# Where attention's last transposes go in PSUM, and behind which copies a gate_up weight's high part is cut, in a hybrid attention block on one core

## The chip, the cores and the metric

The kernel runs on one core of a Trainium2 chip. A core has a matrix engine (PE, whose weight loads are listed apart as PEld), a vector engine (DVE), a scalar engine (ACT), a general engine (POOL), a sync engine that issues DMAs (SP), and 16 DMA engines. PE writes only to PSUM, which has eight banks of 128 partitions by 512 f32; DVE and ACT read it back. Each engine runs its own list of instructions in order and waits for the others by semaphores.

The metric is the device time of one execution in microseconds (us). A number of executions is timed and their median taken; one more execution is recorded by the hardware profiler, and all the rows below come from it.

## What is computed

One layer on x of 1024 rows by 1024 columns, in f32. What matters here is:

```python
q, k, v, f_logit, g_b, g_c, hc, gate_conv, gate_attn = jnp.split(h @ w_in, _SPLITS, axis=-1)
ya = g_b * causal_depthwise_conv(g_c * hc, conv_w)
yb = forgetting_attention(q, k, v, log_sigmoid(f_logit + b_f))   # 8 heads of 64, causal softmax with a bias
merged = sigmoid(gate_conv) * (ya @ w_branch[0]) + sigmoid(gate_attn) * (yb @ w_branch[1])
x = x + rmsnorm(merged @ w_out, norm_mix_post)
h = rmsnorm(x, norm_ffn_pre)
g, u = jnp.split(h @ w_gate_up, 2, axis=-1)
x = x + rmsnorm((silu(g) * u) @ w_down, norm_ffn_post)
```

## The kernel before, in words

**Products.** PE multiplies f32 as three products of split operands: `split(hi, lo, src)` has ACT copy `src` to a rounded high part `hi` and DVE subtract it from `src` to give `lo`; `mm3` then issues high by high, high by low and low by high. The large products (w_in, w_out, gate_up, w_down) are Strassen-Winograd products of seven half-size ones; `prod` is one of them, 12 matmuls of 128x512 for 128 columns of a weight.

**Order.** Up to line 1385 (`strict[0] = ()`) attention runs in the order in which it is written, on all engines: `InOrder` keeps each instruction behind the one written before it on its engine. After that line a planner orders each engine's instructions, by its own times and by priorities. There, `pinned(call, names...)` (line 118) has the instructions that `call` issues on the named engines kept behind whatever was written last before them on the same engine; nothing else is held by it, and instructions written later may still be planned ahead. `ahead(call)` (line 124) raises a priority. All operations pass through one helper, so every row names line 76 and rows are told apart by their tiles.

**Attention.** `steps` (line 898) are 24 steps, each a pair of heads and one or two blocks of 128 query rows; `NU` is 24. Step t multiplies queries and keys into PSUM tiles `sp` (pool `pss`, tag "S", two buffers of two banks, `qk`), DVE adds the bias and takes the row's extreme (`row_max`), and ACT takes the exponential (`expo`, tile `pt`). One step later `turn_bank(back, e, half, engine)` (line 871) transposes the blocks of head e on PE, up to four into one bank of `tps` (tag "T", two buffers of one bank), and returns a `drain`, the copy of that bank to `ptT` by ACT or DVE. After another step or more `pv_pair` multiplies `ptT` with the values into `po`. The remaining two banks are `ma` (holds `po`) and `mb`. Between these, `fill` gives PE matmuls of the other branch (`pba`, `branch_a`): 12 matmuls per tile, all into the one bank `mb`, which DVE empties by a multiplication into `um`. `units` says how many quarters of such a tile each step takes; step 24 takes a whole one. In the loop at line 1278, step 24 has no queries left: it issues `fills()` (12 matmuls, and ACT's high part of a w_branch weight), then the transposes of step 23 (query block 4, five key blocks for each of two heads), and step 25 multiplies steps 22 and 23 with the values.

**w_out's product and the start of gate_up.** From line 1618 the four row pairs i = 0 to 3 of w_out are multiplied (`first`, `second`, `p_s2`, `p_s1`, `p_s3`, `p_s4`, `p_a22`), normalised (`e_norm(i)`, DVE and ACT, which writes `tt` and the tile of `keeps[i]`, named `raw` for i < 3) and transposed (`e_turn(i)`, line 1595: 16 transposes on PE in four banks `tp`, kept in their place behind the PE instruction written before them, and four ACT copies `um<-tp`). `psm` has four banks at this stage, shared by `tp`, `q` and `b3`. `p_s3(i)` ends in an ACT copy `c<-p`, a DVE addition to `c` and an ACT square of it (`junk<-c`). In the last turn of the loop, i = 3, `e_turn(1)` is written right behind `p_s3(3)`.

The first gate_up products are begun in the same stage: `f_begin(n, ...)` (line 1629) loads weight n (`raw`, three buffers, SP's DMA queue), splits it (`prep_first`, line 565) and multiplies it with the first quarter of the turned rows; `f_end(n)` does the second quarter. They are written as begin 0, `e_turn(2)`, begin 1, end 0, begin 2, end 1, begin 3, `e_turn(3)`, end 2, end 3 (lines 1702 to 1711).

Of the kernel before, what the change touches and what calls it, by code (L numbers as in the profile page):

```python
# [10 lines left out]
F32 = mybir.dt.float32  # L11
# [6 lines left out]
P = 128  # L18
S = 1024
# [3 lines left out]
NC = 512  # L23
# [23 lines left out]
def block_kernel(  # L47
# [17 lines left out]
    engines = ("tensor", "vector", "scalar", "gpsimd", "sync")  # L65
# [28 lines left out]
    def pool(name, bufs=1, side="left", space=None):  # L94
        kw = dict(name=name, bufs=bufs)
        if space is not DRAM:
            kw["reuse_waits"] = "tile"
        if space is not None:
            kw["space"] = space
        else:  # L100
            kw["side"] = side
        stack = ExitStack()
        ctx.callback(stack.close)
        return stack.enter_context(tc.tile_pool(**kw)), stack.close

    def f32(ap):
        return ap.bitcast(F32)
# [4 lines left out]
    def sub(o, a, b):  # L112
        nc.vector.tensor_tensor(o, a, b, op=ALU.subtract)
# [4 lines left out]
    def pinned(call, *names):  # L118

        was, strict[0] = strict[0], names  # L120
        call()
        strict[0] = was

    def ahead(call, by=80):
        with tc.high_priority(offset=by):
            call()

    def copy(o, a):
        nc.scalar.activation(o, a, AF.Copy)

    def split(hi, lo, src):

        copy(hi, src)
        sub(lo, src, f32(hi))
# [9 lines left out]
    cpool, _ = pool("const")  # L144
    stat, _ = pool("stat", 4, side="right")
    stat.tile([P, 56], F32, name="pad", bufs=1)
    dpool, _ = pool("dram", space=DRAM)
# [383 lines left out]
    wpool, _ = pool("w")  # L531
# [4 lines left out]
    def kblk(t):  # L536
        return t.rearrange("p (a b) -> p a b", b=P)
# [4 lines left out]
    def raw_t():  # L542
        return wtile("raw", 3)

    def hi_t():
        return wtile("hi", 4, F32R)

    def lo_t():
        return wtile("lo", 3, F32R)
# [10 lines left out]
    def kmaj(src):  # L560
        return src.rearrange("(k p) m -> p k m", p=P)

    LO, UP = slice(0, 4), slice(4, 8)

    def prep_first(src1, there=None):

        if there is None:
            r1 = raw_t()
            nc.sync.dma_start(r1, kmaj(src1))
            h1, l1 = hi_t(), lo_t()  # L570
            split(h1, l1, r1)
        else:
            r1, h1, l1 = there
        return dict(A11=(h1[:, LO], l1[:, LO]), A12=(h1[:, UP], l1[:, UP])), r1
# [113 lines left out]
    def wcols(c0):  # L688
        return win[:, c0 : c0 + P]
# [178 lines left out]
            accum_out=rsums[steps[t][0]][:, c : c + 1],  # L868
        )

    def turn_bank(t, e, half, engine):

        n = sum(i + 1 for i in steps[t][1])
        ks = range(4 * half, min(4 * half + 4, n))
        if not ks:
            return
        if (t, e) not in ptTs:
            ptTs[t, e] = (
                t1.tile([P, ST, P], F32, tag="pT", name="ptT", bufs=6)
                if t  # L880
                else raw_t()
            )
        tps = pss.tile([P, 4, P], F32, tag="T", name="tps", bufs=2)
        for k in ks:
            nc.tensor.transpose(
                tps[:, k - ks[0], :], ps_[t, e][:, k * P : (k + 1) * P], ident
            )
        o, a = ptTs[t, e][:, ks[0] : ks[-1] + 1, :], tps[:, : len(ks), :]

        def drain():  # L890
            if engine == "ACT":
                copy(o, a)
            else:
                nc.vector.tensor_copy(o, a)

        return drain
# [3 lines left out]
    NU = len(steps)  # L900
# [95 lines left out]
    for ij, (kind, j, _, _) in enumerate(jobs):  # L996
        mid = None
        if ij in side:
            cut, store = side.pop(ij)
# [7 lines left out]
        if ij < 2:  # L1007
            if ij == 0:
                r1 = raw_t()
                nc.sync.dma_start(r1, kmaj(wcols(jobs[1][2])))  # L1010
                t0_.tile([P, S], F32, tag="p", name="room", bufs=2)
                h1, l1 = (
                    kblk(t0_.tile([P, S], F32R, tag="cb", name=n, bufs=2)) for n in ("h1", "l1")
                )
# [8 lines left out]
            w = {**w, **prep_rest(wcols(jobs[ij][3]), r1)}  # L1023
            if ij == 1:
                pairs.q.append(pairs.prep(*pairs.srcs.popleft()))
            _, c12, c21, c22 = strassen(w, h1b, psm, pp, p1, mid)
# [7 lines left out]
        else:  # L1034
            w = pairs.get()
            psm_close()
            strict[0] = engines
            pss, pss_close = pool("pss", space=PSUM)
# [11 lines left out]
        elif kind == "gb":  # L1050
            for m, parts in ((j, (c11, c12)), (j + 1, (c21, c22))):
                zt = zts.pop(m)
                for n in range(2):
# [5 lines left out]
                    for t in (1, 0):  # L1059
                        back = 2 - t  # L1060
# [29 lines left out]
    um = um_pool.tile([P, KT, S], F32, name="um")  # L1090
# [78 lines left out]
    def inverse(j):  # L1169

        invs[j] = st_tile("ri", 2 * ST)
        nc.vector.reciprocal(invs[j], rsums[j])
# [78 lines left out]
    cuts, at = defaultdict(list), defaultdict(list)  # L1251
# [32 lines left out]
    for t in range(2, NU + 2):  # L1284
        turned = None
        now = groups(t) if t < NU else ([], [])
        back = t - 1 if t <= NU else None
        wide = back and sum(i + 1 for i in steps[back][1]) > 6
        if t < NU:
            step_qk(t)  # L1290
        if t > 6:
            for u in due(t):
                pv_pair(u)
        if t in rows:
            turned = inverse_rows(rows[t], pst, "mb")
        if t == NU + 1:
            turned = inverse_rows(3, pss, "T", 2)
        lows, muls = [], []

        def fills():  # L1300
            lows.extend(f for f in (g() for g in cuts.pop(t, ())) if f)
            muls.extend(m for m in (next(fill, None) for _ in range(units.get(t, 0))) if m)

        if t == NU:
            fills()
        if back:
            da = turn_bank(back, 0, 0, "ACT")
            db = turn_bank(back, 0, 1, "DVE")
            da()
        if t <= 6:  # L1310
            for u in due(t):
                pv_pair(u)
        for i, e in now[0]:
            row_max(t, i, e)
        if t < NU and len(steps[t][1]) > 1:
            mask_of(t, steps[t][1][1])
        if turned:
            turned()
        if t == NU:
            for f in lows + muls:  # L1320
                f()
            lows, muls = [], []
        if back and db:
            db()
        for i, e in now[0]:
            expo(t, i, e)
        if t == NU:
            inverse(3)
        else:
            fills()  # L1330
        if back:
            dc = turn_bank(back, 1, 0, "ACT" if wide else "DVE")
            dd = turn_bank(back, 1, 1, "DVE" if wide else "ACT")
        for i, e in now[1]:
            row_max(t, i, e)
        if 7 < t < NU:
            for m in muls:
                m()
            muls.clear()
        if t == NU - 1:  # L1340
            for i, e in now[1]:
                expo(t, i, e)
        if back:
            dc()
            if dd:
                dd()
        if t < NU - 1:
            for i, e in now[1]:
                expo(t, i, e)
        if t + 1 < NU:  # L1350
            mask_of(t + 1, steps[t + 1][1][0])
        for f in lows + muls + at.pop(t, []):
            f()
# [241 lines left out]
    def e_turn(i):  # L1595
        for e in range(2):
            st = 2 * i + e
            ss = slice(st * P, (st + 1) * P)
            for q in range(2):
                tp = psm.tile([P, 4, P], F32, tag="mm", name="tp")  # L1600

                def turns():
                    for k in range(4):
                        kt = 4 * q + k
                        nc.tensor.transpose(
                            tp[:, k, :], turned[i][e][:, kt * P : (kt + 1) * P], ident
                        )

                pinned(turns, "tensor")
                ahead(lambda: copy(um[:, 4 * q : 4 * q + 4, ss], tp))  # L1610

    for step in (0, 1, 2, 3):
        first(step)
# [5 lines left out]
    for k in (0, 2):  # L1619
        w = ep.tile([P, D], F32, tag="t", name="wr", bufs=1)  # L1620
        cut_wo(w, ((B22, 4 + k, n2), (B22, 5 + k, n2)))

    def f_src(f):
        return wgu[:, f * P : (f + 1) * P], wgu[:, FH + f * P : FH + (f + 1) * P]

    FIRSTS = [*range(2, NPRE), 0, 1]
    begun, kept = {}, {}

    def f_begin(n, b1, p1):
        f = FIRSTS[n]  # L1630
        w, _ = prep_first(f_src(f)[0])
        prod(b1, w["A11"], hb[B11], True)
        pinned(lambda: copy(p1, b1), *(("scalar",) if n >= 8 else ()))
        if f > 1:
            nc.gpsimd.dma_start(pre_dram[f][0], p1)
        begun[n] = w, b1, p1

    def f_end(n, c11):
        f = FIRSTS[n]
        w, b1, p1 = begun.pop(n)  # L1640
# [82 lines left out]
    def first_tile(n, name, slot):  # L1723
        f = FIRSTS[n]
        return um[:, slot, (n1, n2)[f]] if f < 2 else t_(fp, name)

    for n in range(4, NPRE + 1):
# [6 lines left out]
        if n == 8:  # L1734
            for sl in range(4):
                a = slice(sl * P, (sl + 1) * P)
                b = slice(NC + sl * P, NC + (sl + 1) * P)
# [28 lines left out]
    for f in range(NF):  # L1766
        if f < NPRE:
# [7 lines left out]
            _, g2, u1_, u2 = strassen(rest.get(False), hb, psm, fp, p1, rest.more)  # L1775
# [35 lines left out]
    def cut(t, g):  # L1811

        return t[:, : min(2, NK - 2 * g)]
# [237 lines left out]
```

## Time and profile before

| | us |
|---|---|
| median of 3 executions | 1319.41 |
| lowest and highest of them | 1319.0, 1319.99 |
| the profiled execution | 1319.29 |
| its span, first to last instruction | 1317.2 |

The page of the profile gives the busy time of each engine over the span, and other views of the same recording give single instructions in order of time, the total of waits by engine, and the busy time by stretches of the span. A row of the timeline has the start in us, the length in us, the engine, the operation, the tile written and the tiles read (`out<-in`), the shape, the number of instructions merged in the row, and in brackets the idle time of the engine before it and what ended that. Matmuls are pipelined, so their rows overlap: the time that a matmul costs is the distance to the next start, not its length.

### The profile page before, as it was taken

Reading aid. Unit: us, or ns where it says so; the run is one execution under the profiler, and the core shown is the slowest. Engines: PE = TensorE matmul, PEld = TensorE weight load, DVE = VectorE, ACT = ScalarE, POOL = GpSimd, SP = SyncE. Lnnn points to the kernel's source line nnn. Section 1 sums busy time; section 2 is a strip of 40 time slices with the busy share of each in tenths; the row PEclk is TensorE's granted clock in tenths of the full one; section 3 lists DMA queues with packets and bytes.
Section 4 is the critical chain, followed back from the end, with each engine's and each line's share of the span. In section 5 each row is a group of like instructions: output and inputs, shape, how many; then the busy total and the mean of one; then the engine's idle time right before and its main releaser. Section 6 shows DMA issues by size and latency. Waiting matters only on the chain.

```text
span 1317.2 us, 17978 instructions
## 1 busy us (share of the span) xinstructions
PE 1306.7 (99%) x6710; PEld 1089.5 (83%) x6710; DVE 964.9 (73%) x1514; ACT 556.8 (42%) x895; POOL 142.4 (11%) x271
## 2 busy tenths in 40 slices
PE   9999999999999999999999999999999999999998
PEld 8988888888888888888888888888888888888886
DVE  6974878765656876686798788987766776676685
ACT  6642322243355866514577522322322234444452
POOL 0001000011012212020011021221001110000000
PEclk9999999999999999999999999999999999999999
DMA  6344544555536545465266455553223338866441
GB/s 217 113 120 136 150 123 121 153 164 146 152 120 200 161 144 171 152 232 208 76 228 207 153 168 177 176 184 104 97 88 118 106 111 282 317 249 193 158 168 64
DMA packets 189351, 211.00 MB, mean 160 GB/s; under 512 B 11584, under 2 KB 137600, under 8 KB 189264
## 3 DMA queue, kind: packets, MB, share of 16 engines
q1 hardware_dynamic: 155872, 146.64, 35.6%
q0 software_dynamic: 16496, 54.83, 11.2%
q10 hardware_dynamic: 16896, 8.39, 2.1%
q8 instruction: 52, 0.85, 0.3%
q14 instruction: 35, 0.29, 0.1%
HBM read 151.30 MB, written 58.52 MB: 159 GB/s over the span
## 4 chain that ended last, share of the span: by engine, by line
PE 96%; DVE 2%; ACT 1%; DMA 1%; issue 0%; SPq 0%; DVEq 0%; ACTq 0%
PE b L76 57%; PE pd L76 16%; PE pba L76 3%; PE pbb L76 3%; PE pv L76 3%; PE po L76 3%; PE tps L76 3%; PE p L76 2%; PE sp L76 2%; PE ma L76 1%; PE q L76 1%; PE tp L76 1%; PE mb L76 1%; DMA xt<-in_x_dram 1%; DVE t L76 0%
## 5 line engine op out<-in xcount | busy, mean ns | idle before, releaser
L76 PE MATMUL b<-x,hi 128*128 128x512 f32 x1088 | 335.3, 389 | 0.0
L76 PEld LDWEIGHTS b<-x,hi 128*128 128x128 f32 x1088 | 204.2, 188 | 42.1
L76 PE MATMUL b<-x,lo 128*128 128x512 f32 x544 | 211.7, 389 | 0.0
L76 DVE TENSOR_TENSOR c<-c,b 128x512 f32<-128x512 f32 x193 | 131.5, 681 | 62.2 <-PE b L76 54.7
L76 DVE TENSOR_TENSOR lo<-raw,hi 128x1024 fp32r<-128x1024 f32 x92 | 110.7, 1204 | 76.6 <-PE b L76 66.8
L76 ACT ACTIVATE hi<-raw 128x1024 fp32r<-128x1024 f32 (+1 forms) x99 | 100.6, 1018 | 97.3 <-PE b L76 49.8
L76 PEld LDWEIGHTS b<-x,lo 128*128 128x128 f32 x544 | 102.1, 188 | 21.2
L76 ACT ACTIVATE hi<-sx 128x1024 fp32r<-128x1024 f32 (+1 forms) x43 | 44.8, 1043 | 152.5 <-PE b L76 144.8
L76 ACT ACTIVATE sgf<-c 128x512 f32<-128x512 f32 x31 | 19.6, 633 | 131.9 <-DVE c L76 112.8
L76 DVE TENSOR_TENSOR lo<-sx,hi 128x1024 fp32r<-128x1024 f32 (+1 forms) x43 | 51.5, 1198 | 30.6 <-PE b L76 27.3
L76 DVE TENSOR_TENSOR sx<-raw 128x512 f32<-128x512 f32 x78 | 53.5, 687 | 14.4 <-DMA raw<-in_w_gate_up_dram 7.1
L76 PE MATMUL pd<-hi,lo 128*128 128x512 f32 x160 | 62.3, 389 | 0.0
L76 PE MATMUL pd<-hi 128*128 128x512 f32 x160 | 61.9, 390 | 0.0
L76 PE MATMUL pd<-ghi 128*128 128x512 f32 x148 | 57.6, 390 | 0.0
L76 PE MATMUL pd<-glo,ghi 128*128 128x512 f32 x148 | 57.6, 389 | 0.0
L76 PE MATMUL pd<-ghi,glo 128*128 128x512 f32 x148 | 57.6, 389 | 0.0
L76 PE MATMUL b<-hT34h,lo 128*128 128x512 f32 x136 | 52.9, 389 | 0.0
L76 PE MATMUL b<-hT34h,hi 128*128 128x512 f32 x136 | 52.9, 389 | 0.0
L76 PE MATMUL b<-hT34l,hi 128*128 128x512 f32 x136 | 52.9, 389 | 0.0
L76 PE MATMUL b<-hT12h,hi 128*128 128x512 f32 x136 | 52.9, 389 | 0.0
L76 PE MATMUL b<-hT12l,hi 128*128 128x512 f32 x136 | 52.9, 389 | 0.0
L76 PE MATMUL b<-hT12h,lo 128*128 128x512 f32 x136 | 52.9, 389 | 0.0
(425 smaller groups left out, 3015.4 us busy)
## 6 DMA issues: line engine op xcount, KB each, us to landing
raw<-in_w_gate_up_dram SPq DMA_DIRECT2D x55, 512.0 KB, 3.9
raw<-in_w_in_dram SPq DMA_DIRECT2D x35, 512.0 KB, 4.3
a_dramS<-um POOLq DMA_DIRECT2D x44, 256.0 KB, 3.0
a_dramA<-um POOLq DMA_DIRECT2D x33, 256.0 KB, 2.7
sg<-sg_dram SPq DMA_DIRECT2D x32, 256.0 KB, 3.9
x<-wo_dram SPq DMA_DIRECT2D x16, 512.0 KB, 5.8
graw<-a_dramS SPq DMA_DIRECT2D x14, 512.0 KB, 4.4
sg_dram<-c POOLq DMA_DIRECT2D x24, 256.0 KB, 3.4
```

Source lines behind the costliest of these rows:

```text
L76: ins = getattr(self.engine, name)(*args, **kw)
```

## The change

Two things are changed. In step 24 of attention the transposes of step 23 are written ahead of the 12 matmuls of `fills()`; for each head their two banks are the two halves of a tile of the tag "S" and no longer two tiles of the tag "T"; all four copies are written behind `fills()`; DVE's reciprocal (`inverse(3)`) is written behind them, and the multiplication that empties `mb` and the low part of the w_branch weight behind that. In w_out's stage, the four copies of `e_turn(1)` are pinned on ACT, and so is the split of gate_up's weight n = 1 (its high part alone is on ACT).

```diff
-    def prep_first(src1, there=None):
+    def prep_first(src1, there=None, cut=split):
...
-            split(h1, l1, r1)
+            cut(h1, l1, r1)
...
-    def turn_bank(t, e, half, engine):
+    def turn_bank(t, e, half, engine, at_=None):
...
-        tps = pss.tile([P, 4, P], F32, tag="T", name="tps", bufs=2)
+        if at_ is None:
+            tps = pss.tile([P, 4, P], F32, tag="T", name="tps", bufs=2)
+        else:
+            tps = at_[:, half].rearrange("p (a b) -> p a b", a=4)
...
         if t == NU:
+            lasts = []
+            for e, engines in enumerate((("ACT", "DVE"), ("DVE", "ACT"))):
+                two = pss.tile([P, 2, NC], F32, tag="S", name="tps2", bufs=2)
+                lasts += [turn_bank(back, e, half, eng, two) for half, eng in enumerate(engines)]
             fills()
+            for f in lasts:
+                f()
+            inverse(3)
+            for f in muls + lows + at.pop(t, []):
+                f()
+            continue
...
-        if t == NU:
-            for f in lows + muls:
-                f()
-            lows, muls = [], []
...
-        if t == NU:
-            inverse(3)
-        else:
-            fills()
+        fills()
...
-                ahead(lambda: copy(um[:, 4 * q : 4 * q + 4, ss], tp))
+                pinned(
+                    lambda: ahead(lambda: copy(um[:, 4 * q : 4 * q + 4, ss], tp)),
+                    *(("scalar",) if i == 1 else ()),
+                )
...
+    cuts_ = {1: lambda *a: pinned(lambda: split(*a), "scalar")}
...
-        w, _ = prep_first(f_src(f)[0])
+        w, _ = prep_first(f_src(f)[0], cut=cuts_.get(n, split))
```

## The prediction

> **What bounds the kernel now.** I read the page first, then busy time by stretches, then PE's waits, then the timeline of each engine around the two places that the diff touches.
>
> ```profile
> span 1317.2 us, 17978 instructions
> ...
> PE 1306.7 (99%) x6710; PEld 1089.5 (83%) x6710; DVE 964.9 (73%) x1514; ACT 556.8 (42%) x895; POOL 142.4 (11%) x271
> ```
>
> ```profile
> 646.00:700.00 54.00, 53.47 (x267) 44.20 (x266) 49.82 (x86) 38.72 (x76) 9.70 (x18) 1.00 0.66 223
> 700.00:1101.00 401.00, 401.00 (x1771) 332.12 (x1770) 310.18 (x441) 129.46 (x177) 55.19 (x102) 1.00 0.43 139
> ```
>
> ```profile
> PE tps L76 <- ACT ptT L76: 0.6, 1, 0.6
> PE tp L76 <- ACT um L76: 0.5, 1, 0.5
> ```
>
> PE is busy for 1306.7 of 1317.2 us. The columns of a stretch are its length, then busy time of PE, PEld, DVE, ACT, POOL, and the granted clock, which is 1.00. From 700 to 1101 us PE never stands. So the end is PE's list of matmuls plus the few places where it stands, and whatever is saved or lost ahead of 700 us arrives at the end undiminished. The two waits sit exactly where the diff is: transposes of attention that wait for a drain by ACT, and turned rows that wait for ACT's copy. The whole of it is one or two us, so this is an account of tenths.
>
> **Part 1: the last transposes.** PE, in order of time:
>
> ```profile
> 530.83 0.88 PE L76 MATMUL tps<-ident,pt 128*128 128x128 f32 x6
> 531.46 0.48 PE L76 MATMUL pba<-yh,s4h 128*128 128x512 f32 x1
> ...
> 534.32 0.82 PE L76 MATMUL tps<-ident,pt 128*128 128x128 f32 x6
> 535.26 0.50 PE L76 MATMUL pba<-yh,s4h 128*128 128x512 f32 x1
> ...
> 538.12 0.71 PE L76 MATMUL tps<-ident,pt 128*128 128x128 f32 x5
> 539.40 0.77 PE L76 MATMUL tps<-ident,pt 128*128 128x128 f32 x5 [0.58 <-ACT ptT L76]
> 540.10 2.62 PE L76 MATMUL po<-ptT,v 128*64 128x128 f32 x44
> ...
> 542.68 0.47 PE L76 MATMUL pba<-yh,s4h 128*128 128x512 f32 x1
> ```
>
> From the last transposes of step 22 (534.32) to the matmuls of step 25 (542.68) PE takes 8.36 us. Two stands lie in it. The 12 `pba` matmuls could not begin until DVE had emptied the single bank `mb` (six transposes elsewhere take 0.63 us to the next matmul, 530.83 to 531.46; here it is 0.94). And the five transposes of the second head waited for the drains of the first, since the tag "T" has two banks: 1.28 us from 538.12 to 539.40 for five transposes.
>
> After the change the list is: 6 transposes, 10 transposes, 12 `pba`, 44 `po`. By starts: 0.63 for the six; ten at 0.63/6 = 0.105 each, 1.05; the twelve 2.86 (535.26 to 538.12); the forty-four 2.58 (540.10 to 542.68). Sum 7.12, gain 1.24. With the slowest pace for transposes in these rows, 0.70 for five (539.40 to 540.10), ten cost 1.40 and the gain is 0.89. If only the idle time that the rows name goes, it is 0.58 and the 0.12 between the end of the transposes (534.32 + 0.82) and 535.26, 0.70 in all. I take 1.0, between the two paces, and keep 0.7 to 1.24.
>
> The Trainium skill, page Perfetto Trace Analysis, section on the Tensor Engine instruction, says that a matmul's end is estimated by the profiler and only its start observed; by that the idle column is a lower bound and the sum by starts the right one. By the idle column the first part would give 0.7, by starts 0.9 to 1.24; no row here decides between them.
>
> What could take the place of these stands? DVE and ACT at that time:
>
> ```profile
> 534.07 0.19 ACT L76 ACTIVATION_READ_ACCUMULATOR pt<-pt,nm 128x1 f32 x1
> ...
> 535.45 1.05 ACT L76 ACTIVATE hi<-raw 128x1024 fp32r<-128x1024 f32 x1
> ```
>
> ```profile
> 534.51 0.69 DVE L76 TENSOR_TENSOR um<-sg,pba 128x512 f32<-128x512 f32 x1 [1.61 <-PE pba L76]
> ...
> 536.32 0.68 DVE L76 TENSOR_TENSOR yb<-yb,rb 128x512 f32<-128x512 f32 x1
> ```
>
> The new transposes need step 23's exponentials. The last ends at 534.26; PE gets there at 534.32 + 0.63 = 534.95, so the cover of the 12 matmuls isn't needed. The two "S" tiles were freed by DVE even earlier, ahead of those exponentials. `mb` is empty at 535.20, the `pba` matmuls now start near 536.0: that stand goes. The drains are written behind the high part of the w_branch weight: ACT ends it at 536.50 and copies two banks by 537.4; DVE ends its division at 537.0 and copies its two by 537.9, then the reciprocal. `po` needs them at 538.9 or later: a cover of one us; without it each tenth would be PE's. What is late next is DVE's multiplication out of `mb`, which now waits for the `pba` matmuls behind the reciprocal, at 539.1 to 539.8; `mb` is wanted again at 541.7, and behind it on DVE stand one low part (1.2 us) and a division (0.7), done by 541.7, when the turned reciprocals arrive. One DMA is issued about a us later, the gate's second half, which takes the buffer that this multiplication frees; its first reader is a sigmoid behind step 25. Everything behind moves forward with PE.
>
> **Part 2: the weight's high part.** PE, then ACT, then DVE:
>
> ```profile
> 654.31 1.03 PE L76 MATMUL tp<-ident,raw 128*128 128x128 f32 x8
> ...
> 656.06 0.70 PE L76 MATMUL p<-x,hi 128*128 128x512 f32 x2
> ...
> 669.80 1.03 PE L76 MATMUL tp<-ident,raw 128*128 128x128 f32 x8
> ...
> 671.79 0.66 PE L76 MATMUL tp<-ident,tt 128*128 128x128 f32 x4 [0.53 <-ACT um L76]
> 672.21 0.71 PE L76 MATMUL p<-x,hi 128*128 128x512 f32 x2
> ...
> 683.82 1.06 PE L76 MATMUL tp<-ident,tt 128*128 128x128 f32 x8
> ```
>
> ```profile
> 669.71 1.07 ACT L76 ACTIVATE hi<-raw 128x1024 fp32r<-128x1024 f32 x1 [3.11 <-DMA raw<-in_w_gate_up_dram]
> 670.68 0.57 ACT L76 ACTIVATE c<-p 128x512 f32<-128x512 f32 x1
> 671.15 2.05 ACT L76 ACTIVATE um<-tp 128x512 f32<-128x512 f32 x4
> 673.06 0.66 ACT L76 ACTIVATE junk<-c 128x512 f32<-128x512 f32 x1
> ...
> 684.49 1.09 ACT L76 ACTIVATE um<-tp 128x512 f32<-128x512 f32 x2
> ```
>
> ```profile
> 670.81 1.23 DVE L76 TENSOR_TENSOR lo<-raw,hi 128x1024 fp32r<-128x1024 f32 x1
> 671.95 0.68 DVE L76 TENSOR_TENSOR c<-c,b 128x512 f32<-128x512 f32 x1
> ...
> 679.08 1.22 DVE L76 TENSOR_TENSOR lo<-raw,hi 128x1024 fp32r<-128x1024 f32 x1
> ...
> 685.28 1.28 DVE L76 SCALAR_TENSOR_TENSOR keep<-keep,r,gpo 128x1024 f32<-128x1024 f32 x1
> ...
> 688.28 0.74 DVE L76 SCALAR_TENSOR_TENSOR tt<-c,r,gpo 128x512 f32<-128x512 f32 x1
> ```
>
> ACT's list had the high part of weight 1 ahead of `c<-p` and the copies of `e_turn(1)`. Its DMA landed at 669.7, so the copies were late; with `b3` in one of the four banks, the fourth group of transposes had to wait for the first copy. The same 16 transposes took 1.75 us for pair 0 (654.31 to 656.06) and 2.41 for pair 1 (669.80 to 672.21): the stand is 0.53 by the row, 0.66 by starts.
>
> Two new orders follow from the pins, by what is written last before each. The copies of `e_turn(1)` come behind the square `junk<-c`; it ran behind them. It waits for DVE's addition to `c`, and that for `c<-p`: about 670.0 to 670.5 for the copy, 670.8 to 671.5 for the addition, the square to 672.1, the first `um` copy to 672.6, where it ended near 671.65. So if PE's list stayed as it is, the fourth group would start 0.9 later than before: the worst of this step, +0.9. I don't take that. `p_s4(3)` and `p_a22(3)`, 24 matmuls of 2.86/12 = 0.24, are written behind the transposes and are not pinned; they need `c<-p` and the addition, both now earlier. And what the planner has to foresee is now a chain of ACT and DVE operations and no DMA; it was the DMA that came late. I take -0.5, the row, and keep -0.66 to +0.9.
>
> The high part of weight 1 comes behind the last copy of `e_turn(2)`, not of `e_turn(1)`: that is the ACT instruction written before it. So it moves from 669.71 to about 685.6, its low part on DVE from 670.81 to 686.6 at best, done at 687.8, and the 12 matmuls of begin 1 cannot start before that. From the end of `e_turn(2)`'s transposes (683.82 and 1.06) PE has to be fed for 2.9 us. End 0 and begin 2 are 24 matmuls, 5.7 us, and weight 2 is split at 680.3: they cover it, if the planner puts them there; if not, that is the slower rival. ACT's 1.07 and DVE's 1.23 leave a stretch where DVE is busy for 49.82 of 54 us and come back a little later in the same stretch: nothing net. Weight 1 holds its `raw` buffer 16 us longer, so the next load on SP goes to the buffer that weight 2 frees at 680.3, and lands well before begin 3, four products later. I take nothing for all of this, with 0 to +2.9 as bounds.
>
> Sum: 1.0 and 0.5 saved, 1.5. The profiled execution took 1319.29, so 1317.8; it lies 0.12 below the median, so the median goes to **1317.9**.
>
> **The rivals.** *The second part gives its half us back.* The transposes of `e_turn(2)` follow closely on DVE's normalised rows; a PE that comes earlier waits there, if no matmul is put in between. For it: DVE's 92% of the stretch. Against: 24 matmuls are free to go there. Then only part 1 counts: 1318.4.
>
> *Slower: begin 1 stays right behind `e_turn(2)`.* PE then stands from 684.9 until weight 1 has its low part. If that queues on DVE behind `e_norm(3)`'s four operations (685.28 to 689.0), it is done at 690.1: 5.2 lost against 1.5, 1323.1. From a stand of 1.5 us on, a low part later than 686.4, the change is a loss; at 687.8 it ends at 1320.8. For it: the pin reaches further than the stall it cures. Against: a planner that knows the pin also knows that begin 1 is not ready.
>
> *The change does not do what it says.* The first stand stays because the drains come later than I think, on ACT or DVE; then PE waits in front of `po` and part 1 keeps half: 1318.4 with the second part, 1318.9 without it.
>
> *The clock falls.* Sixteen transposes now stand in a row in attention. If PE's clock went to half, the 12 `pba` behind them would cost 2.86 more: 1320.8. Against it: `e_turn(0)`'s sixteen stand in a row at 654.31, in a stretch with granted clock 1.00. The Trainium skill, page TensorE: Matmul & The Clock Gate, section "Part 4: PE-mode transpose", says that transposes do not count as busy PE time for the clock; by that rule a longer run of them is a risk, and the trace speaks against it at this length.
>
> **How the numbers follow.** Forecast 0.56; gives back 0.22; slower 0.08, over half of that by more than 0.2%; not what it says 0.07; clock 0.02; and 0.05 that small gaps at `e_turn(2)` and `e_turn(3)` go as well, to 1317.0 or a little lower. A measurement of this kernel can tell 0.2%, 2.6 us, from no change: below 1316.8 or above 1322.05. Faster by that 0.03, since all the stands that the diff can reach add up to less; within it 0.92; slower 0.05. The range goes from 1317.0, where the upper bounds of both parts and the small gaps meet, to 1319.7, where part 2 loses its 0.9 and part 1 keeps little; outside are the stand behind `e_turn(2)` and the clock.
>
> **What would show it.** Right: no wait of `tps` for `ptT` on PE, ten transposes ahead of the `pba` matmuls, and step 25's `pba` about 1.0 us earlier; no wait of `tp` for `um`; `um<-tp` of pair 1 behind `junk<-c` on ACT, matmuls of `p` or `b` between the groups of those transposes; weight 1's high part behind the copies of `e_turn(2)`. Wrong: a stand of PE in front of `po`, or in front of the `b` matmuls between 684 and 690 us, or PE idle beyond 700.

## The result: 1326.4 us, 6.8 us slower

| | before | after |
|---|---|---|
| median, measured side by side | 1319.59 (6 runs) | 1326.38 (6 runs) |
| lowest and highest after | | 1324.53, 1328.99 |
| the profiled execution | 1319.29 | 1326.32 |
| its span | 1317.2 | 1324.3 |

The ratio is 1.0052, with an interval of 1.0042 to 1.0062: slower, by more than twice what a measurement here can tell. The forecast was 1317.9, and the range ended at 1319.7.

The stretches of the changed kernel (columns as before), and PE's waits in them (us in total, times, longest):

```profile
646.00:700.00 54.00, 51.22 (x254) 41.56 (x253) 45.03 (x79) 35.18 (x69) 8.61 (x16) 1.00 0.62 207
700.00:1101.00 401.00, 397.57 (x1748) 328.64 (x1747) 309.70 (x440) 130.80 (x180) 55.73 (x103) 1.00 0.42 136
```

```profile
PE b L76 <- ACT c L76: 3.4, 1, 3.4
...
PE b L76 <- DVE x L76: 1.4, 1, 1.4
...
PE b L76 <- ACT sx L76: 0.7, 1, 0.7
...
PE b L76 <- DVE lo L76: 0.4, 1, 0.4
PE b L76 <- DVE c L76: 0.3, 1, 0.3
```

Neither wait that the change was aimed at (`tps` for `ptT`, `tp` for `um`) is left. In their place stand five others, all of `b`: the fourth product of pair 3 (`p_s4`, from the 0.3 for `c`) and the first products of gate_up. The largest lies beyond 700 us, where PE had not stood once before (700 to 1101 us).

**Part 1 did what it says.** PE in attention, and the granted clock (the column of 1.00) around it:

```profile
534.36 1.91 PE L76 MATMUL tps<-ident,pt 128*128 128x128 f32 x16
536.02 0.48 PE L76 MATMUL pba<-yh,s4h 128*128 128x512 f32 x1
...
538.93 2.62 PE L76 MATMUL po<-ptT,v 128*64 128x128 f32 x44
...
541.52 0.47 PE L76 MATMUL pba<-yh,s4h 128*128 128x512 f32 x1
```

```profile
534.00:536.00 2.00, 2.00 (x19) 1.87 (x18) 1.44 (x3) 1.09 (x4) 0.00 (x0) 1.00 0.00 0
536.00:539.00 3.00, 3.00 (x17) 2.25 (x17) 2.10 (x5) 1.31 (x3) 0.00 (x0) 1.00 0.42 134
```

From the transposes to step 25 it is now 541.52 - 534.36 = 7.16 us, against 8.36: 1.20 saved, with no stand and no fall of the clock. PE is still that far ahead when pair 1's transposes begin (668.63 against 669.80).

**Part 2 lost it seven times over.** PE from there on; the rows around each stand:

```profile
670.64 0.62 PE L76 MATMUL p<-x,hi 128*128 128x512 f32 x2
671.54 0.72 PE L76 MATMUL b<-x,s4h 128*128 128x512 f32 x2 [0.28 <-DVE c L76]
...
676.46 0.39 PE L76 MATMUL b<-x,hi 128*128 128x512 f32 x1
678.25 0.50 PE L76 MATMUL b<-x,hi 128*128 128x512 f32 x1 [1.40 <-DVE x L76]
...
680.65 0.39 PE L76 MATMUL b<-x,lo 128*128 128x512 f32 x1
681.72 0.50 PE L76 MATMUL b<-x,hi 128*128 128x512 f32 x1 [0.69 <-ACT sx L76]
...
686.93 0.65 PE L76 MATMUL b<-x,hi 128*128 128x512 f32 x2
687.99 0.50 PE L76 MATMUL b<-x,lo 128*128 128x512 f32 x1 [0.42 <-DVE lo L76]
...
710.53 0.39 PE L76 MATMUL b<-x,lo 128*128 128x512 f32 x1
714.34 1.05 PE L76 MATMUL b<-x,hi 128*128 128x512 f32 x2 [3.43 <-ACT c L76]
...
718.10 0.63 PE L76 MATMUL b<-x,hi 128*128 128x512 f32 x2
```

Read by starts: two matmuls from 670.64 should take 0.45 and took 0.90, a loss of 0.45. In the same way 676.46 to 678.25 loses 1.56, 680.65 to 681.72 loses 0.84, 686.93 to 687.99 loses 0.61 and 710.53 to 714.34 loses 3.58 (at 0.227 us per matmul, the pace of the rows without a stand). From 714.34 to 718.10 nine matmuls take 3.76 us, not 2.04: another 1.72. That stretch has this clock (the last but two column):

```profile
714.00:716.00 2.00, 1.66 (x4) 1.30 (x5) 2.00 (x4) 1.83 (x4) 0.54 (x1) 0.64 1.05 349
716.00:718.00 2.00, 2.00 (x6) 1.56 (x5) 2.00 (x5) 0.71 (x3) 0.54 (x1) 0.50 0.55 218
```

All losses together are 8.76. Less the 1.20 of part 1 and the 0.66 of the stand that was cured, that makes 6.90; the two profiled executions differ by 7.03. So the account is closed to a tenth or two, and what is left is why each stand is there. ACT and then DVE of the changed kernel:

```profile
671.98 0.61 ACT L76 ACTIVATE junk<-c 128x512 f32<-128x512 f32 x1
...
672.59 2.04 ACT L76 ACTIVATE um<-tp 128x512 f32<-128x512 f32 x4
674.50 2.02 ACT L76 ACTIVATE x<-um 128x1024 fp32r<-128x1024 f32 x2
...
682.70 2.20 ACT L76 ACTIVATE um<-tp 128x512 f32<-128x512 f32 x4 [1.03 <-PE tp L76]
684.77 2.01 ACT L76 ACTIVATE hi<-raw 128x1024 fp32r<-128x1024 f32 x2
...
690.60 0.60 ACT L76 ACTIVATE sx<-b 128x512 f32<-128x512 f32 x1
...
712.57 0.63 ACT L76 ACTIVATE x<-sx 128x512 fp32r<-128x512 f32 x1 [1.00 <-DVE sx L76]
713.18 0.63 ACT L76 ACTIVATE x<-w 128x512 fp32r<-128x512 f32 x1
713.71 0.58 ACT L76 ACTIVATE c<-b 128x512 f32<-128x512 f32 x1
```

```profile
676.98 2.36 DVE L76 TENSOR_TENSOR x<-um,x 128x1024 fp32r<-128x1024 f32 x2
...
686.72 1.22 DVE L76 TENSOR_TENSOR lo<-raw,hi 128x1024 fp32r<-128x1024 f32 x1
...
688.99 2.36 DVE L76 TENSOR_TENSOR lo<-raw,hi 128x1024 fp32r<-128x1024 f32 x2
...
698.67 0.69 DVE L76 TENSOR_TENSOR sx<-um 128x512 f32<-128x512 f32 x1 [1.82 <-DMA pre_dram<-sx]
```

The copies of pair 1 stand behind the square, as pinned. Behind them come the splits of these rows (`x<-um`), whose low part DVE begins at 676.98, and begin 0 waits for it at 678.25. At 684.77 two high parts run in a row: that of weight 1, as pinned, and that of weight 2, which nobody pinned. Before, weights 2 and 3 were cut here:

```profile
676.62 1.07 ACT L76 ACTIVATE hi<-raw 128x1024 fp32r<-128x1024 f32 x1
...
678.61 1.07 ACT L76 ACTIVATE hi<-raw 128x1024 fp32r<-128x1024 f32 x1
...
685.46 0.61 ACT L76 ACTIVATE sx<-b 128x512 f32<-128x512 f32 x1
...
706.48 0.60 ACT L76 ACTIVATE c<-b 128x512 f32<-128x512 f32 x1
708.51 0.63 ACT L76 ACTIVATE x<-sx 128x512 fp32r<-128x512 f32 x1 [1.43 <-DVE sx L76]
```

```profile
691.21 0.68 DVE L76 TENSOR_TENSOR sx<-um 128x512 f32<-128x512 f32 x1
```

The row at 685.46 is the copy of begin 1's first half (`p1`); it is now at 690.60. DVE's first sum of the turned rows (`sx<-um`) takes the tile of that copy, waits until its store has landed, and starts at 698.67, where it was 691.21. The splits of the sums are late with it. The copy of begin 4 (the product written next behind `end 3`) was at 706.48, ahead of the splits of the third set of sums (708.51); now it stands in ACT's list behind the first two of these (712.57 and 713.18), at 713.71. PE waits for that copy at 714.34. This is a chain read from rows; the experiments test its links.

### The profile page after: what moved, and what is told of

It reads as the page before. It is cut to its first block, busy times and chain, and to the rows that moved or that the text cites. A ratio compares the mean times of both kernels' runs of the same rounds, so it can differ in the third digit from the quotient of the medians.

```text
span 1324.3 us, 17975 instructions
## 1 busy us (share of the span) xinstructions
PE 1308.4 (99%) x6710; PEld 1089.7 (82%) x6710; DVE 965.5 (73%) x1514; ACT 557.7 (42%) x895; POOL 142.3 (11%) x271
## 4 chain that ended last, share of the span: by engine, by line
PE 93%; DVE 4%; ACT 1%; DMA 1%; issue 1%; SPq 0%; DVEq 0%; ACTq 0%
PE b L76 55%; PE pd L76 16%; PE pba L76 3%; PE pbb L76 3%; PE pv L76 3%; PE tps L76 3%; PE po L76 3%; PE sp L76 2%; PE p L76 2%; PE ma L76 1%; PE q L76 1%; DVE lo L76 1%; PE mb L76 1%; DVE x L76 1%; DMA pre_dram<-sx 1%
```

## The experiments

Every time is a median, beside the kernel before on the same chip (1319.57, 1319.53, 1319.56 and 1319.62 in the four sets of runs). The intervals reach about 1.3 us to each side, so a difference of one us or less rests on the rows beside it and not on the times alone.

### One part at a time

Part 1 alone: the pins are gone.

```diff
-                    *(("scalar",) if i == 1 else ()),
+                    *(),
...
-    cuts_ = {1: lambda *a: pinned(lambda: split(*a), "scalar")}
+    cuts_ = {}
```

> Step 24 of attention as in the changed kernel, nothing pinned in w_out's stage. All theories: the transposes' part is sound and saves what it saved in the changed kernel (step 25's first pba matmul 1.16 us earlier), the loss lies in the pins. Median 1.0 to 1.3 us below the kernel before, about 1318.3. If the loss came from attention's part after all, this one would be near 1326.

Measured: 1318.48 over 11 runs, ratio 0.9991 (0.9982 to 1.0): 1.1 us less, close to the 1.20 of the rows. PE still waits for `um` at 671.00, for 0.75.

The pins alone, in the kernel before:

> Both pins, attention as before. If the parts simply add, this is the slowest of all: 1326.4 + 1.2 = 1327.6, 8 us above the kernel before, with the same stand of PE of about 3.4 us behind the begun products and the granted clock near half behind it. If the pins only lose together with attention's earlier end, it is at 1320 or below.

Measured: 1327.53 over 4 runs, ratio 1.006 (1.0046 to 1.0073): 8.0 more. Less the 1.1 of part 1 that is 6.9, and the change measures 6.8: the two parts add up, and the whole loss is the pins'. The stand beyond 700 us is there too (3.58 at 716.49), but without the half clock.

Part 1 with the copies' pin alone, and part 1 with the weight's pin alone:

```diff
-    cuts_ = {1: lambda *a: pinned(lambda: split(*a), "scalar")}
+    cuts_ = {}
```

> Attention as changed, only the four copies of e_turn(1) pinned. Theory 'weight' (the pinned high part of weight 1 makes begin 1 late, and with it everything that waits for its sx half): this one loses only the stand of PE for the half split of the turned rows, 1.4 to 1.6 us, against the 0.6 that it cures, about 1319 to 1320. Theory 'copies' (the copies behind the square delay the half splits, begin 0 and all after): 1324 or more.

```diff
-                    *(("scalar",) if i == 1 else ()),
+                    *(),
```

> Attention as changed, only the split of weight 1 pinned. Theory 'weight': most of the loss, 1323 to 1326, with the stand of about 3.4 us near 714 us and a first sx<-um of DVE that waits for the store of sx. Theory 'copies': 1318 to 1319, and no wait of PE for the turned rows' copies.

Measured: 1319.67 over 10 runs, ratio 1.0001 (0.9992 to 1.001), for the copies' pin; 1323.74 over 7 runs, ratio 1.0029 (1.0019 to 1.004), for the weight's, with one execution at 1320.64 and the others from 1323.04 to 1324.58. Against part 1 alone that is +1.2 and +5.3; both together are +7.9, so 1.4 comes from their meeting. With the copies' pin the stand for `x` at 679 is there (0.79) and none at 714. With the weight's pin there is none at 714 either, so that one shows only where both pins are; PE's stand is elsewhere:

```profile
685.15 0.64 PE L76 MATMUL b<-x,hi 128*128 128x512 f32 x2
689.36 0.73 PE L76 MATMUL b<-x,hi 128*128 128x512 f32 x2 [3.57 <-ACT hi L76]
```

The high part that it waits for starts at 688.25, when the load of that weight has landed: a load that was issued at 681.17, when PE had read pair 2's rows out of a buffer `raw` (its transposes, 680.03 and 1.06). In the kernel before, the load behind weight 2's was issued at 672.06, as soon as DVE had subtracted weight 1 (670.81 and 1.23) and freed its buffer; with the pin that buffer is held until 686.66. So the weight's pin delays not one weight, but those behind it too.

### Is it the order of the weights?

Weight 2's tiles are taken, and its load and split written, ahead of `e_turn(2)`, so ahead of the pinned weight 1; all else is as in the change.

```diff
     begin_early(0)
+    raw_t()
+    early_w[2] = prep_first(f_src(FIRSTS[2])[0])[0]
     e_turn(2)
...
-        w, _ = prep_first(f_src(f)[0], cut=cuts_.get(n, split))
+        w = early_w.pop(n, None) or prep_first(f_src(f)[0], cut=cuts_.get(n, split))[0]
...
-        if f == 2:
-            raw_t()
```

> The change with one edit: weight 2's tiles are taken, and its load and split written, ahead of e_turn(2) and so ahead of the pinned weight 1. Theory (weight 2 fell behind weight 1 because their tiles are handed out in written order): the high part of weight 2 runs before 672 us and no longer right behind weight 1's at 685.8; begin 2 then has matmuls ready between 684 and 688 us and the stand there for a weight's low part (0.42 us by the row, 0.6 by starts) goes; begin 1 is still late and the stand at 714 stays, so only 0.5 to 1.5 is won: 1325.2, within 1324.5 and 1326. Rival (the planner had other reasons): weight 2's high part stays behind weight 1's, time 1326.4.

Measured: 1322.63 over 6 runs, ratio 1.0027 (1.0016 to 1.0038). The mechanism is as expected (ACT, below: weight 2's high part is back ahead of 672, no wait for a `lo` is left), and the gain, 3.75, is far above the 0.5 to 1.5 expected: the stand at 714 shrinks too, and the half clock behind it is gone. That is the profiled execution, 1321.9; three of the six took 1323.25 to 1325.13, and what they lose isn't recorded.

```profile
668.29 1.06 ACT L76 ACTIVATE hi<-raw 128x1024 fp32r<-128x1024 f32 x1 [3.04 <-DMA raw<-in_w_gate_up_dram]
```

```profile
711.59 0.73 PE L76 MATMUL b<-x,hi 128*128 128x512 f32 x2 [1.75 <-ACT c L76]
```

The same edit with the weight's pin alone:

```diff
-                    *(("scalar",) if i == 1 else ()),
+                    *(),
```

> As the run before, but p1 of begin 0 and begin 1 stays in the tile that DVE's sums use next. Theory: DVE's first sum still waits for the store of p1 to land (696 us or later), PE stands 1 to 2 us near 711 for the copy of begin 4, and the time is 1 to 2.5 above the run before: 1319.8 to 1321.5; against the pin alone (1323.74) the order of the weights is worth 2 to 4. Rival (the tile of p1 costs nothing once weight 2 comes first): both runs within 0.7 of each other.

Measured: 1320.17 over 10 runs, ratio 1.0004 (0.9994 to 1.0013). Against the pin alone (1323.74) the order of the weights is worth 3.6 of the 5.3. ("The run before" in the expectation is the one with tiles of their own for p1, shown under the next heading.) The time is within what was expected, but the stand is not there: in the profiled execution, 1319.39 and the lowest of the ten, PE does not stand near 711, although DVE's first sum is late:

```profile
700.00:1101.00 401.00, 401.00 (x1770) 331.71 (x1769) 311.74 (x443) 130.28 (x178) 55.35 (x102) 1.00 0.43 140
```

```profile
697.74 0.69 DVE L76 TENSOR_TENSOR sx<-um 128x512 f32<-128x512 f32 x1 [1.13 <-DMA pre_dram<-sx]
```

### The link through the tile of p1

In the change, the results of begin 0 and begin 1 get tiles of their own:

```diff
-    sx = flat(wtile("sx", 1))
-    early = [sx[:, n1], sx[:, n2], t_(fe, "c22"), t_(fe, "c22")]
+    early = [f32(flat(s4h_t())), f32(flat(s4h_t())), t_(fe, "c22"), t_(fe, "c22")]
```

> The change with one edit: the first halves' results of begin 0 and begin 1 (p1) are copied to two tiles of the tag s4h and no longer to the tile of the tag sx that DVE's sums use next. Theory (the late begin 1 holds DVE's sums through that tile until its store has landed, 698.67 us): DVE's first sum starts before 692 us, PE's stand of 3.43 us at 714 for the copy of begin 4 is under 1 us, the half clock behind it is gone, and the time is about 3.6 + 1.7 = 5 below the change's 1326.4: 1321.1, within 1320.3 and 1322.3. The stands between 678 and 690 us stay. Rival (ACT and DVE are behind by themselves after the late splits): the stand at 714 keeps more than 2 us and the time stays above 1324.5.

Measured: 1325.94 over 4 runs, ratio 1.0048 (1.0035 to 1.0062). Half of the theory held: the first sum starts at 684.13, and the stand at 714 falls to 0.74. But the time did not: PE stands earlier, for a high part that ACT starts at 689.15, when its load has landed, again with a half clock behind it. DVE now takes the sum ahead of the low part of weight 1 (688.39, where it was 686.72 in a trace that runs 0.8 earlier); how the one leads to the other is not shown.

```profile
687.73 0.65 PE L76 MATMUL b<-x,hi 128*128 128x512 f32 x2
690.26 0.73 PE L76 MATMUL b<-x,hi 128*128 128x512 f32 x2 [1.89 <-ACT hi L76]
```

```profile
691.20:694.61 3.41, 3.41 (x10) 2.61 (x9) 3.10 (x5) 2.09 (x5) 1.07 (x2) 0.50 0.84 219
```

And with the weight's pin alone and weight 2 first:

> Part 1, and the pin on weight 1's split alone (the copies of e_turn(1) are free), with weight 2's tiles taken ahead of e_turn(2) and with tiles of their own for p1 of begin 0 and begin 1. Theory (the weight's pin costs 5.3 us only by what it drags along: weight 2 behind it, and DVE's sums behind the store of the late p1): with both links cut no stand of PE over 0.7 us is left between 678 and 720 us, the clock stays at 1.00, and the time is 1318.0 to 1320.0. Rival (12 matmuls of begin 1 and ACT's and DVE's late splits cost by themselves): stands of 2 us or more in sum between 684 and 716 us, time 1321.5 or more.

Measured: 1320.77 over 10 runs, ratio 1.001 (1.0001 to 1.002), 0.6 above the same kernel with p1 in the old tile (1320.17). No stand is above 0.7 and the clock stays, but the time misses its range by 0.8, and the rival named for the pair holds: once weight 2 comes first and the copies are free, the tile of p1 costs nothing that the times can tell. That link carries the delay in the changed kernel; it isn't its source.

### The last link: ACT's list ahead of the copy of begin 4

In the change, the high parts of the second set of sums are held behind that copy:

```diff
+        if n == 4:
+            p1_copy.append(nc.scalar.activation(p1, b1, AF.Copy))
...
+        def cut(hi, lo, src):
+            h = nc.scalar.activation(hi, src, AF.Copy)
+            if sl == 1:
+                tc.add_manual_dep(h.ins, p1_copy[0].ins.name, ...)
+            sub(lo, src, f32(hi))
...
-            split(hb[o][0][:, :, a], hb[o][1][:, :, a], t)
+            cut(hb[o][0][:, :, a], hb[o][1][:, :, a], t)
```

> The change with one edit: the high parts of the second set of sums (x from sx and w) are held behind the copy of begin 4 on ACT, so that copy no longer stands behind them. Theory (end 4 waits only because that copy is queued behind splits whose sums are late): the stand of 3.43 us at 714 is under 1 us, the half clock of 3.41 us behind it is gone, time 1321.1, within 1320.3 and 1322.3. Rival (the copies of the next products are queued behind the same late sums): the stand moves to the copy of begin 5 or 6 and keeps more than 2 us, time above 1324. Rival (the clock falls without a stand): the stand goes but a half clock stays, 1322.5 to 1323.5.

Measured: 1322.44 over 10 runs, ratio 1.0022 (1.0012 to 1.0031): 3.9 less than the change, and 0.1 above the range. The stand is 1.10, not under 1, and no half clock follows. So 3.9 of the 6.8 hang on the order around this copy in ACT's list, stand and clock together. The edit moves more than the copy: in the changed kernel it was the third set's splits that stood right ahead of it, and the second set's were through by 709.9; now the sums in `sx` of both sets are split behind the copy, the second's from 711.74 on.

```profile
711.91 0.73 PE L76 MATMUL b<-x,hi 128*128 128x512 f32 x2 [1.10 <-ACT c L76]
```

### A pin that ends where the stall ended

Part 1, free copies, and weight 1's high part behind the last copy of `e_turn(1)`, not of `e_turn(2)`:

```diff
+                    last_um[i] = nc.scalar.activation(um[:, 4 * q : 4 * q + 4, ss], tp, AF.Copy)
...
+    def cut_behind(hi, lo, src):
+        h = nc.scalar.activation(hi, src, AF.Copy)
+        tc.add_manual_dep(h.ins, last_um[1].ins.name, ...)
+        sub(lo, src, f32(hi))
+
+    cuts_ = {1: cut_behind}
```

> Part 1 as in the change; the copies of e_turn(1) are not pinned, and the high part of weight 1 has to stand behind the last copy of e_turn(1) and nothing later. Theory (the place of the pin was wrong, not its aim): the transposes' stand for um at 671 (0.75 us with part 1 alone) goes, no stand takes its place between 678 and 690 us nor at 714, begin 1's p1 copy ends before 687 us, and the time is 0.5 to 0.8 below part 1 alone (1318.48): 1317.8, within 1317.3 and 1318.3. Rival (the gain is given back at e_turn(2) or by the two copies' order): 1318.3 to 1319.0. Rival (any move of weight 1's split costs, since ACT and DVE are full here): above 1320.

Measured: 1319.70 over 11 runs, ratio 1.0003 (0.9995 to 1.0012). The stand for `um` is gone and nothing stands from 678 to 690 or at 714, but the gain is given back, and more, in front of `e_turn(3)`:

```profile
697.90 1.06 PE L76 MATMUL tp<-ident,keep 128*128 128x128 f32 x8 [1.67 <-DVE keep L76]
```

The same with `e_turn(3)` six matmuls later:

```diff
-    e_turn(3)
     end_early(2)
+    e_turn(3)
```

> As the run with weight 1's high part right behind e_turn(1) (1319.70), with e_turn(3) written behind end 2 and no longer ahead of it, so that its transposes stand behind all 12 matmuls of end 2 on PE instead of behind the first 6. Theory (that run gave its gain back in one stand of 1.67 us in front of e_turn(3), whose rows DVE had not normalised): six matmuls are 1.37 us, the stand falls to 0.3 us or goes, and the time is 1.2 to 1.7 lower: 1318.2, within 1317.8 and 1318.6, at or a little below part 1 alone (1318.48). Rival (DVE's rows or sums become late by as much again): a stand of 1 us or more at another place, time 1319.3 or more.

Measured: 1319.05 over 11 runs, ratio 0.9996 (0.9987 to 1.0005). That stand is gone and the only one left in the stage is 0.21, yet the median is between the two expectations, 0.65 below the run before it and 0.6 above part 1 alone. The profiled execution, 1318.22, is the lowest of the 11, so it doesn't show what the others lose. Of all these kernels, part 1 alone has the lowest median, though 0.6 is less than the times alone can tell.

## Why the prediction was wrong

**Part 1 was right.** 1.0 was taken, from bounds of 0.7 to 1.24; the rows show 1.20 and the medians 1.1 (a time alone would leave it at the edge: the interval of the ratio ends at 1.0). The sum by starts (1.24, ten transposes at 0.105) was nearer than the cautious middle. The Trainium skill, page Perfetto Trace Analysis, section on the Tensor Engine instruction, has starts as the observed side; the 1.20 agrees, and the 0.7 of the idle column is too little for these rows. The drains were in time, the last with 0.7 us to spare and not one (ACT's second copy, 537.99 and 0.28): `po` starts 0.32 behind the last `pba` (538.61), the gap that such a change of operation has elsewhere in these rows.

**The copies' pin: the step was followed one engine too short.** "The first `um` copy to 672.6" meant its end; in the row it starts then (672.59), since ACT took the 1.06 us of `raw<-xt` ahead of the square. The transposes' stand is gone and matmuls fill the place, as said. But the step stopped at the fourth group of transposes, and closed with -0.5. Who reads these copies was not asked: the splits `x<-um`, then begin 0. Their first low part moved from 675.01 to 676.98 on DVE, and PE, now earlier, met it one matmul behind 676.46. The pin measures +1.2 against part 1 alone, beyond even the +0.9 named as its worst.

**The weight's pin: "End 0 and begin 2 are 24 matmuls ... they cover it" failed.** The term was taken as nothing, with 0 to +2.9 as bounds; alone it measures +5.3 against part 1 alone. The step took the split of weight 2 from the trace of before and left it there, with "if the planner puts them there" as the only doubt. In the changed kernel weight 2 was cut behind weight 1, at 685.8, with its low part behind 689.0, and weight 3 behind both. Neither its data nor ACT kept weight 2 back: its load was issued at 669.69 and moved its last packet at 674.62, and ACT stood for 1.16 us ahead of 681.07, longer than a high part takes (1.06). Begin 2 was as late as begin 1. End 0, for its part, had been pulled forward to follow begin 0, where it waits for its `p1` copy (0.84 by starts). Taking weight 2's tiles first brings 3.75 back in the change and 3.6 with the pin alone: the weights are held in the order in which they are written. That it is their tiles that do so, and not the written place of load and split, which moved with them, is argued, not shown. "Lands well before begin 3" failed by the same step: with the pin alone, the stand is at a weight that waited for its load.

**Weight 1 itself came as foreseen:** low part "done at 687.8" at best, 687.94 in the row, and a stand of 0.61 in its place. The slower rival, which had a chance of 0.08, saw the late low part of weight 1 as the loss, 5.2 and 1323.1. Its sign was right, its place wrong: more than half of the loss is 26 us behind, at a copy on ACT that does not read the weight.

**"Whatever is saved or lost ahead of 700 us arrives undiminished"** was read from a stretch in which PE never stood. That says that it had no stand at that timing, not that the other engines had room. Begin 1's `p1` copy was 5.1 late (685.46 to 690.60); the first sum became 7.5 late, the copy of begin 4, now behind two of the third set's splits and no longer ahead of them, 7.2, and PE stood 3.58. The sign that the prediction named, "PE idle beyond 700", is what showed it.

**The clock** fell, but not for the rival's reason: sixteen transposes in a row left it at 1.00.

What is not settled: why the copy of begin 4 falls behind the late splits in the changed kernel and not in the kernel with the weight's pin alone and weight 2 first, where DVE's sum is nearly as late (697.74 against 698.67) and PE does not stand there: in that one the copy is at 708.50, ahead of the third set's splits (710.37), as in the kernel before and with either pin alone, where PE doesn't stand either. With both pins it is behind them, also without part 1 (715.86 behind 714.72) and with weight 2 first (710.96 behind 709.82), and PE stands. The order that the planner gave ACT differs between them; no run isolates it from the rest.

## What to carry to other kernels

A pin that cures a stall also holds whatever shares a ring of buffers or a written order with the pinned instruction; before taking the next product as cover, check that its operands do not stand in that order. Follow a delayed result through its readers until one of them is early enough, on every engine, and count a result that holds a shared tile or waits for a store as late by that as well. An engine that never stands in the trace of before shows nothing of the slack of those that feed it.

## What the runs showed of the hardware

A stand of PE can cost more than itself. Behind the 3.43 us at 714.34 and the 3.57 us at 689.36 (the weight's pin alone) the granted clock was 0.50 for 3.41 us by the clock's own record, 1.7 us of work each. The Trainium skill, page TensorE: Matmul & The Clock Gate, section "What's actually happening", gives this length for a free-running window, and half speed after about one idle window. The length agrees. The condition does so less: 1.89 us was enough at 690.26, and a longer stand, in the kernel with the pins alone, left the clock at 1.00:

```profile
716.49 0.74 PE L76 MATMUL b<-x,hi 128*128 128x512 f32 x2 [3.58 <-ACT c L76]
```

The clock's own record shows where the windows lie: up to the half clock, the clock is full for 709.97, 682.67 and 686.08 us in the three kernels that have one, which is 208, 200 and 201 times 3.413 us. Counted off in the same way, the stand of 3.58 us falls into two windows and the one of 1.89 us into one (the length, then PE's busy time; the clock is the last but two column). First the kernel with the pins alone, then the change with tiles of their own for p1, whose next window is the one at 0.50 shown above:

```profile
711.41:714.82 3.41, 1.50 (x7) 0.93 (x5) 3.41 (x6) 1.36 (x4) 0.48 (x1) 1.00 0.64 213
714.82:718.23 3.41, 1.74 (x7) 1.42 (x8) 3.41 (x7) 3.24 (x6) 0.59 (x2) 1.00 0.75 229
```

```profile
687.78:691.20 3.42, 1.53 (x7) 0.96 (x7) 3.42 (x5) 2.05 (x4) 0.53 (x1) 1.00 0.76 249
```

So of two stands of nearly one length, the 3.57 us that left one window idle for 2.79 was followed by half clock, and the 3.58 us that left 1.91 and 1.67 was not. What idle share of a window is enough is not settled: 1.75 in one window (weight 2 first) was not, 1.89 was, and 1.91 was not. These busy times rest on modelled ends, which may well hide 0.02 us; a limit near 1.9 of the 3.41 us is an estimate from these rows, and no run varies the length or the place of a stand by itself.
